# The gate's sums over partitions moved from TensorE to VectorE and a row in DRAM, and casts of late weights put behind the copies of ended banks

## The chip, the core and the metric

The kernel runs on one core of one Trainium2 chip. The metric is device time in microseconds (us) for one execution of the whole kernel. The time before is 908.64 us, the median of 3 runs (908.38 to 908.87).

## The reference

One layer of a decoder trunk is computed in float32 for a sequence of 256 tokens, 2048 model channels and a branch of 4096 channels. Written out for this case (a batch of one, one layer):

```python
h = rmsnorm(x, norm_g)                                # x: 256 x 2048
shift, scale, gate = split(silu(c) @ ada_w + ada_b, 3)  # c: 2048; ada_w: 2048 x 6144
h = h * (1 + scale) + shift
b, cg, v, g = split(h @ sc_w_in, 4)                   # sc_w_in: 2048 x 16384
u = causal_depthwise_conv(cg * v, sc_conv_w)          # three taps
y = (b * u * silu(g)) @ sc_w_out                      # sc_w_out: 4096 x 2048
out = rmsnorm(x + gate * y, final_g)
```

The vector `gate` (2048 numbers) is needed only at the end, where the output product is scaled by it. `shift` and `scale` are needed at the start, channel by channel.

## The kernel before

**Products.** Each float32 matrix is split into a high part in TensorE's reduced float32 type and the low rest, and each product is three matmuls: high by high, high by low, low by high. ScalarE makes the high part of a piece of weights (a cast, L616 in the first half of the kernel, L357 in `split` later), VectorE subtracts it from the raw piece and so makes the low part (L625, later L358). A piece is 128 x 2048 elements, 1 MB. Its raw, high and low tiles have three buffers each, so a cast waits until TensorE is through with the piece three before it.

**First half (channels 0 to 2047 of the branch, tiles `mm_s`).** `silu(c) @ ada_w` comes in pieces too, and the 16 blocks of 128 channels of `h` become ready two by two. The function `plan` (L77) writes out by hand which chunk (`ch`, 0 to 3) and which quarter (`q`, 0 to 3) of the projection is multiplied by which channels. A pass over two chunks fills two banks of PSUM, and there are three bank tiles in turn, so TensorE can begin a bank only when the bank three before it has been copied out. `keep` (L547) empties a bank: by a copy on ScalarE (L551) where it is the first part of the sum, else by an addition on VectorE (L553). The tile `acc03` holds chunk 0 and quarter 3. A loop over the pieces with a model of each engine's clock writes the program; until all of `h` is ready each engine's instructions stand in the order in which this loop issues them. For piece `b` it calls `close_bank` for the last bank that has ended and `high(b + 2)` (the cast two pieces ahead). `early` (L758) sets which of the two comes first. `low(b + 2)` (L770 or L802) follows, then the matmuls of the piece, and between a pass's two banks `close_bank` for the first (L795).

**Sums over partitions.** VectorE multiplies rows of `ada_w` by `silu(c)` and adds them up (`gv`, L484 and L486); what is left is a sum over the 128 partitions. Groups that begin at channel block 2 and 4 are turned by TensorE (`ada_turn`, L493) and summed on VectorE. Groups from 6 on are turned in 32 x 32 blocks by VectorE, summed, brought side by side and summed again (L503 to L509).

**Second half (channels 2048 to 4095, tiles `mm_b`).** Here the gate is computed beside the products, for its four parts of 512 columns one after the other (`dc`, 0 to 3). Every second piece of weights is followed by a load of a piece of `ada_w` (`gate_piece`, L834), and `gate_summed` (L855) multiplies and adds it into `gacc` on VectorE. After a part's last piece the sum over partitions is a matmul with a matrix of ones (`ones_e`), which leaves every partition with the whole sum: ScalarE takes the high part (L868), VectorE the low part (L869), TensorE runs two matmuls of 512 columns (L871), and VectorE adds the result to the bias in `gate` (L872). These instructions are traced with a later priority, and those on VectorE stand behind the low part of the next piece.

**Output stage (tiles `mm_o`).** The product with `sc_w_out` runs over four parts of 512 columns; the first three are scaled by `gate` after the product (L994), and for the fourth the weights are scaled before (L978).

Of the kernel before, what the change touches and what calls it, by code (L numbers as in the profile page):

```python
# [13 lines left out]
P = 128  # L14
# [51 lines left out]
TURN_US = 0.5  # L66
PE_TURNS = 6
TOTAL_US = 2.95
# [8 lines left out]
def plan():  # L77
# [36 lines left out]
    while new or any(k < KT for k in done.values()):  # L114
        before = []
        hi = sum(r <= pe for r in ready)
        if new:
            p = new.pop(0)
            k0 = done[p] = 0
            if p not in order:  # L120
                del done[p]
                done[order[0]] = hi
        else:
            old = [p for p in order if done[p] < KT]
            p = old[0] if hi == KT else min(old, key=lambda p: done[p])
# [30 lines left out]
def short_conv_layer(ctx: ExitStack, tc: tile.TileContext, x, c, norm_g, ada_w, ada_b, w_in, conv_w, w_out, final_g, out):  # L156
# [317 lines left out]
    def ada_sums(k0, nk, piece, at4):  # L474
# [5 lines left out]
        for i in range(kk):  # L480
# [4 lines left out]
            else:  # L485
                nc.vector.scalar_tensor_tensor(out=gv, in0=at4[:, i], scalar=c_k, in1=gv, op0=ALU.mult, op1=ALU.add)  # L486

    def ada_turn(k0, nk):

# [6 lines left out]
    def ada_total(k0, nk, tp):  # L496

        if tp is not None:
            gs = const.tile([P, 2, nk], F32, tag="gs", name="gs", bufs=2)
            nc.vector.reduce_sum(gs.rearrange("p s k -> p (s k)"), tp, axis=mybir.AxisListType.X)  # L500
            return gs[:, 0], gs[:, 1]
        tp = psum.tile([P, 512], F32, tag="sm", name="tp_g", bufs=2)
        nc.vector.transpose(tp, sums[k0].rearrange("p s f -> p (s f)"))  # L503
        nc.vector.reduce_sum(by_block, tp.rearrange("p (b j) -> p b j", j=32), axis=mybir.AxisListType.X)
        for g in range(4):
            nc.vector.tensor_copy(out=side[:, g, :], in_=by_block[32 * g : 32 * g + 32, :])
        gs = const.tile([P, 2, nk], F32, tag="gs", name="gs", bufs=2)
# [136 lines left out]
    def turn_sums(by):  # L644

        while turning and turning[0][0] < PE_TURNS and turning[0][2] <= by:
            k0, nk, _ = turning.pop(0)
            totals.append((k0, nk, ada_turn(k0, nk), clock["pe"]))

    def total_sums():  # L650

        while totals:
# [4 lines left out]
            spend("dve", FOLD_US, at)  # L657
        while turning and turning[0][0] >= PE_TURNS:
            k0, nk, _ = turning.pop(0)
# [92 lines left out]
    for b, (n, chs, q, k0, k1, seeds, w, s0, sk, _) in enumerate(flat):  # L752
# [6 lines left out]
        for closing in (early, not early):  # L759
# [4 lines left out]
            else:  # L764
                nxt = b + 2 < N and high(b + 2)
        get_ready(s0 + sk)
        if nxt:
            sum_some(nxt[2] + STALL_US, HI_US)
            if not turning or turning[0][0] >= PE_TURNS:
                low(b + 2, *nxt)  # L770
                nxt = None
# [9 lines left out]
        for j in range(len(chs)):  # L781
# [9 lines left out]
            if j == 0:  # L791
# [38 lines left out]
    gate_todo = [(dc, j) for dc in range(4) for j in range(0, KT, 2)]  # L830
    gate_held = []
    gacc = [None]
# [10 lines left out]

    def gate_sums():
        if not gate_held:
            return
        traced = nc.cur_bb.bb.instructions
        n = len(traced)
        with later(GIVE):
            gate_summed(*gate_held.pop(0))  # L850
        for ins in list(traced[n:]):
# [3 lines left out]
    def gate_summed(dc, j, at3):  # L855
# [9 lines left out]
        if j + 2 == KT:  # L865
            ps = psum.tile([P, 512], F32, tag="sm", name="ps_gate", bufs=2)
            parts = adap.tile([P, 2, 512], F32R, tag="at", name="gate_s", bufs=4)
            nc.scalar.copy(parts[:, 0], ga)  # L868
            nc.vector.tensor_tensor(out=parts[:, 1], in0=ga, in1=parts[:, 0].bitcast(F32), op=ALU.subtract)  # L869
            for i in range(2):  # L870
                nc.tensor.matmul(ps, ones_e, parts[:, i], start=i == 0, stop=i == 1)  # L871
            nc.vector.tensor_tensor(out=gate(dc), in0=ps, in1=gate(dc), op=ALU.add)  # L872

    KP = 8
    n_piece = 0
    for ct in range(NS, NCT, 2):
        for q in QUARTERS:
            bank = psum.tile([P, CT, T], F32, tag=in_turn(), bufs=1, name="mm_b")[:, 0:2]
            col = q * E + ct * P
            for kp in range(0, KT, KP):  # L880
# [12 lines left out]
                n_piece += 1  # L893
                if n_piece % 2:
                    gate_piece()
                else:
# [59 lines left out]
    for dc in range(4):  # L956
# [10 lines left out]
        for ep in range(n_ep):  # L967
# [7 lines left out]
            if dc == 3:  # L975
# [4 lines left out]
                )  # L980
            hi, lo = split(raw, SLOT, "raw")
            out_mm(po[0], 0, ep, hi, lo)
            if dc == 3 and ep >= n_ep - LATE:
# [53 lines left out]
```

## Time and profile before

| what | number |
|---|---|
| median of 3 runs | 908.64 us |
| time of the profiled execution | 908.68 us |
| span of it, first to last instruction | 906.9 us |
| TensorE busy | 893.4 us, 99% |
| VectorE busy | 643.5 us, 71% |
| ScalarE busy | 448.3 us, 49% |
| GpSimd busy | 1.8 us |
| bytes read from HBM | 224.48 MB |
| mean granted TensorE clock | 0.999 |

PE is TensorE's matmuls, PEld its weight loads, DVE is VectorE, ACT ScalarE, POOL GpSimd and SP SyncE, which issues nearly all loads. The time of a run is somewhat longer than the span, here by 1.78 us. A matmul's row gives the time from its start to its modelled end, and matmuls overlap; what one costs TensorE is read from the distance to the next start. "Idle before" with an arrow tells how long the engine had nothing to do and what ended that.

### The profile page before, as it was taken

What the parts mean: (1) busy time and instruction counts of PE and PEld (TensorE: products, weight loads), DVE (VectorE), ACT (ScalarE), POOL (GpSimd) and SP (SyncE); (2) the same over time, 40 slices, a digit from 0 to 9 for tenths busy, and PEclk for the clock granted to TensorE, in tenths of its full rate; (3) what the DMA queues carried; (4) which work ended last, traced back from release to release, by engine and by line L of the source; (5) the groups of instructions that cost most, each with busy time, mean ns of one, the idle gap of its engine ahead of it and who ended that gap; (6) DMA issues with size and microseconds to landing.
All of it is one profiled execution on the core that took longest, in us unless ns stands there. A gap on an engine that the chain in (4) does not pass through costs nothing.

```text
span 906.9 us, 16139 instructions
## 1 busy us (share of the span) xinstructions
PE 893.4 (99%) x7025; PEld 856.7 (94%) x7025; DVE 643.5 (71%) x653; ACT 448.3 (49%) x381; POOL 1.8 (0%) x8
## 2 busy tenths in 40 slices
PE   7999999999999999999999999999999999999996
PEld 4999999999999999999999999999999988888885
DVE  5788989989966868776666665657666644555882
ACT  6688755655446745544443343444333443443333
POOL 0000000000000000000000000000000000000000
PEclk9999999999999999999999999999999999999999
DMA  9999999898955566787787778777877496555542
GB/s 308 387 379 331 327 322 360 288 323 320 325 190 185 188 222 197 246 285 240 221 269 242 242 223 263 235 242 236 258 234 234 144 364 205 202 200 186 186 139 93
DMA packets 146855, 227.62 MB, mean 251 GB/s; under 512 B 5457, under 2 KB 103905, under 8 KB 146401
## 3 DMA queue, kind: packets, MB, share of 16 engines
q1 hardware_dynamic: 146688, 226.56, 74.6%
q8 instruction: 55, 0.90, 0.4%
q14 instruction: 16, 0.12, 0.0%
q0 software_dynamic: 64, 0.02, 0.0%
q10 hardware_dynamic: 32, 0.01, 0.0%
HBM read 224.48 MB, written 2.10 MB: 250 GB/s over the span
## 4 chain that ended last, share of the span: by engine, by line
PE 94%; DMA 4%; ACT 1%; SPq 0%; ACTq 0%; issue 0%; DVE 0%
PE mm_b L519 38%; PE mm_s L519 36%; PE mm_o L934 6%; PE mm_o L933 6%; PE mm_o L935 6%; DMA at<-in_ada_w_dram 3%; DMA raw_s<-in_sc_w_in_dram 1%; DMA x<-in_x_dram 1%; ACT hi L616 0%; PE ps_gate L871 0%; ACT acc L551 0%; PE tp_g L493 0%; SPq L591 0%; ACT big L947 0%; ACT big L944 0%; ACTq L1033 0%
## 5 line engine op out<-in xcount | busy, mean ns | idle before, releaser
L519 PE MATMUL mm_b<-hT,hi 128*128 128x256 f32 x2048 | 348.4, 276 | 0.0
L519 PE MATMUL mm_s<-hT,hi 128*128 128x256 f32 x2048 | 346.0, 277 | 0.6 <-ACT acc L551 0.6
L519 PEld LDWEIGHTS mm_b<-hT,hi 128*128 128x128 f32 x2048 | 308.5, 188 | 0.1
L519 PEld LDWEIGHTS mm_s<-hT,hi 128*128 128x128 f32 x2048 | 306.0, 188 | 1.0 <-ACT acc L551 0.8
L519 PE MATMUL mm_b<-hT,lo 128*128 128x256 f32 x1024 | 282.6, 276 | 0.0
L519 PE MATMUL mm_s<-hT,lo 128*128 128x256 f32 x1024 | 277.3, 276 | 0.0
L358 DVE TENSOR_TENSOR lo<-raw,hi 128x2048 fp32r<-128x2048 f32 x64 | 146.7, 2292 | 114.8 <-ACT hi L357 114.8
L357 ACT CAST hi<-raw 128x2048 fp32r<-128x2048 f32 x64 | 122.4, 1913 | 197.7 <-PE mm_b L519 145.6
L519 PEld LDWEIGHTS mm_b<-hT,lo 128*128 128x128 f32 x1024 | 192.2, 188 | 0.0
L519 PEld LDWEIGHTS mm_s<-hT,lo 128*128 128x128 f32 x1024 | 189.8, 188 | 0.0
L625 DVE TENSOR_TENSOR lo<-raw_s,hi 128x2048 fp32r<-128x2048 f32 (+1 forms) x65 | 145.3, 2239 | 38.1 <-ACT hi L616 38.0
L616 ACT CAST hi<-raw_s 128x2048 fp32r<-128x2048 f32 (+1 forms) x65 | 121.5, 1873 | 90.7 <-PE mm_s L519 70.2
L358 DVE TENSOR_TENSOR lo<-raw_o,hi 128x2048 fp32r<-128x2048 f32 x32 | 73.3, 2291 | 62.7 <-ACT hi L357 62.6
L357 ACT CAST hi<-raw_o 128x2048 fp32r<-128x2048 f32 x32 | 61.0, 1907 | 106.4 <-PE mm_o L935 84.5
L934 PE MATMUL mm_o<-lo,y 128*128 128x512 f32 x256 | 99.3, 389 | 0.0
L935 PE MATMUL mm_o<-hi,y 128*128 128x512 f32 x256 | 99.3, 389 | 0.0
L933 PE MATMUL mm_o<-hi,y 128*128 128x512 f32 x256 | 99.3, 389 | 0.0
L486 DVE SCALAR_TENSOR_TENSOR gv<-at,silu_c,gv 128x512 f32<-128x512 f32 x105 | 78.8, 750 | 3.0 <-DMA at<-in_ada_w_dram 0.3
L935 PEld LDWEIGHTS mm_o<-hi,y 128*128 128x128 f32 x256 | 48.0, 188 | 10.1
L933 PEld LDWEIGHTS mm_o<-hi,y 128*128 128x128 f32 x256 | 48.0, 188 | 10.0
L934 PEld LDWEIGHTS mm_o<-lo,y 128*128 128x128 f32 x256 | 48.0, 188 | 9.8
L551 ACT COPY acc<-mm_s 128x1024 f32<-128x1024 f32 x46 | 46.3, 1016 | 7.9 <-PE mm_s L519 7.8
(109 smaller groups left out, 373.8 us busy)
## 6 DMA issues: line engine op xcount, KB each, us to landing
raw<-in_sc_w_in_dram SPq DMA_DIRECT2D x64, 1024.0 KB, 6.4
raw_s<-in_sc_w_in_dram SPq DMA_DIRECT2D x63, 1024.0 KB, 7.1
raw_o<-in_sc_w_out_dram SPq DMA_DIRECT2D x32, 1024.0 KB, 5.1
at<-in_ada_w_dram SPq DMA_DIRECT2D x126, 256.0 KB, 7.4
at_g<-in_ada_w_dram SPq DMA_DIRECT2D x32, 512.0 KB, 7.5
x<-in_x_dram SPq DMA_DIRECT2D x4, 512.0 KB, 6.6
big<-in_x_dram SPq DMA_DIRECT2D x2, 1024.0 KB, 7.8
out_dram<-big SPq DMA_DIRECT2D x4, 512.0 KB, 2.9
```

The lines of the kernel that those rows point to most:

```text
L357: nc.scalar.copy(hi[:, :n], raw[:, :n])
L358: last_low[0] = nc.vector.tensor_tensor(out=lo[:, :n], in0=raw[:, :n], in1=hi[:, :n].bitcast(F32), op=ALU.subtract)
L486: nc.vector.scalar_tensor_tensor(out=gv, in0=at4[:, i], scalar=c_k, in1=gv, op0=ALU.mult, op1=ALU.add)
L519: mm = last_mm[0] = nc.tensor.matmul(dst, w, h[:, k], start=begins and left, stop=ends, skip_group_check=True)
L551: nc.scalar.copy(acc[ch, q], bank)
L616: nc.scalar.copy(hi[:, h], raws[b][:, h])
L625: nc.vector.tensor_tensor(out=lo[:, h], in0=raw[:, h], in1=hi[:, h].bitcast(F32), op=ALU.subtract)
L933: nc.tensor.matmul(po, yh, hi[:, o], start=opens, stop=False, skip_group_check=True)
L934: nc.tensor.matmul(po, yh, lo[:, o], start=False, stop=False, skip_group_check=True)
L935: nc.tensor.matmul(po, yl, hi[:, o], start=False, stop=ct == NCT - 1, skip_group_check=True)
```

## The change

Three things are changed.

The gate's sum over partitions no longer goes through TensorE. `block_sums`, the code that stood in `ada_total` for groups from 6 on, now also takes `gacc`: VectorE turns it in 32 x 32 blocks, sums each row of a block, and puts the four groups of partitions side by side. One more reduction (32 x 16) and one more transpose (32 x 32) leave the 512 sums as 16 rows of 32. GpSimd's queue writes these to a row in DRAM (`row`) and reads the row back into all 128 partitions (`gate_w`). The addition to `gate` is a separate step, `gate_add`, issued three pieces of weights later at the earliest (for the last part, in the output stage).

In the loop of the first half, a piece whose load is expected (by the loop's own clock) only after the first bank of the present pass has ended is marked `far`. Its cast and its low part are then issued behind the copy of that ended bank, not ahead of it.

`PE_TURNS` becomes the list (2, 4), and the plan's rule uses the number 8 where it had `PE_TURNS + 2`.

```diff
-PE_TURNS = 6
+PE_TURNS = (2, 4)
...
-            seed = k0 > 0 and (act < dve or pieces and hi > PE_TURNS + 2)
+            seed = k0 > 0 and (act < dve or pieces and hi > 8)
...
+    drams = ctx.enter_context(tc.tile_pool(name="drams", bufs=2, space=bass.MemoryType.DRAM))
...
+    total = rows1[0:32, 16:48]
+    total_t = rows1[0:32, 80:112]
...
+    def block_sums(gv):
+
+        tp = psum.tile([P, 512], F32, tag="sm", name="tp_g", bufs=2)
+        nc.vector.transpose(tp, gv)
+        nc.vector.reduce_sum(by_block, tp.rearrange("p (b j) -> p b j", j=32), axis=mybir.AxisListType.X)
+        for g in range(4):
+            nc.vector.tensor_copy(out=side[:, g, :], in_=by_block[32 * g : 32 * g + 32, :])
...
-                nxt = b + 2 < N and high(b + 2)
+                far = b + 2 < N and raws.get((b + 2, "at"), begin) > begin + us / len(chs)
+                nxt = b + 2 < N and not far and high(b + 2)
...
+                if far:
+                    nxt = high(b + 2)
+                    sum_some(nxt[2] + STALL_US, HI_US)
                 if nxt:
                     low(b + 2, *nxt)
...
-            ps = psum.tile([P, 512], F32, tag="sm", name="ps_gate", bufs=2)
-            parts = adap.tile([P, 2, 512], F32R, tag="at", name="gate_s", bufs=4)
-            nc.scalar.copy(parts[:, 0], ga)
-            nc.vector.tensor_tensor(out=parts[:, 1], in0=ga, in1=parts[:, 0].bitcast(F32), op=ALU.subtract)
-            for i in range(2):
-                nc.tensor.matmul(ps, ones_e, parts[:, i], start=i == 0, stop=i == 1)
-            nc.vector.tensor_tensor(out=gate(dc), in0=ps, in1=gate(dc), op=ALU.add)
+            block_sums(ga)
+            nc.vector.reduce_sum(total_t[:, 0:16], side.rearrange("p g b -> p b g"), axis=mybir.AxisListType.X)
+            nc.vector.transpose(total, total_t)
+            row = drams.tile([512], F32, tag="row", name="row")
+            nc.gpsimd.dma_start(row.rearrange("(b i) -> b i", b=16), total[0:16, :])
+            whole = adap.tile([P, 512], F32, tag="gv", name="gate_w")
+            nc.gpsimd.dma_start(whole, row.partition_broadcast(P))
+            gate_whole.append((dc, whole, n_piece))
+
+    def gate_add():
+
+        dc, whole, _ = gate_whole.pop(0)
+        nc.vector.tensor_tensor(out=gate(dc), in0=whole, in1=gate(dc), op=ALU.add)
```

Where this moves instructions is shown in three places.

ScalarE, near the start, before: CAST rows make the high part of a piece of weights, COPY rows empty a bank into `acc` (the two digits are chunk and quarter). `raw_s_308` is the raw tile of piece 5, `raw_s_341` that of piece 6.

```order
L551 COPY acc02_408<-mm_s_343 128x1024
L551 COPY acc12_435<-mm_s_344 128x1024
L616 CAST hi_437<-raw_s_308 128x2048
L551 COPY acc03_483<-mm_s_383 128x1024
L551 COPY acc13_510<-mm_s_410 128x1024
L616 CAST hi_512<-raw_s_341 128x2048
L551 COPY acc00_548<-mm_s_458 128x1024
L551 COPY acc10_575<-mm_s_485 128x1024
```

The same place after; piece 5 is now `raw_s_335` and piece 6 `raw_s_369`.

```order
L558 COPY acc02_398<-mm_s_339 128x1024
L623 CAST hi_401<-raw_s_292 128x2048
L558 COPY acc12_437<-mm_s_340 128x1024
L558 COPY acc03_464<-mm_s_373 128x1024
L623 CAST hi_467<-raw_s_335 128x2048
L558 COPY acc13_512<-mm_s_400 128x1024
L558 COPY acc00_539<-mm_s_439 128x1024
L623 CAST hi_542<-raw_s_369 128x2048
L558 COPY acc10_577<-mm_s_466 128x1024
```

One copy has moved ahead of each of these casts: `acc03` ahead of the cast of piece 5, `acc00` ahead of that of piece 6 (and, likewise, `acc02` ahead of piece 4 and `acc22` ahead of piece 8). Behind piece 9 the order of ScalarE's early part is as before.

TensorE, before, at the sum of the gate's first part: two matmuls of 512 columns stand among those of the second half.

```order
L519 MATMUL mm_b<-hT,lo 128x256
L519 MATMUL mm_b<-hT,hi 128x256 x2
L871 MATMUL ps_gate<-gate_s,ones 128x512
L519 MATMUL mm_b<-hT,lo 128x256
L871 MATMUL ps_gate<-gate_s,ones 128x512
L519 MATMUL mm_b<-hT,hi 128x256 x2
```

The same place after.

```order
L526 MATMUL mm_b<-hT,lo 128x256
L526 MATMUL mm_b<-hT,hi 128x256 x2
L526 MATMUL mm_b<-hT,lo 128x256
L526 MATMUL mm_b<-hT,hi 128x256 x2
L526 MATMUL mm_b<-hT,lo 128x256
```

The two `ps_gate` rows are gone, here and for the other three parts; nothing else on TensorE has moved.

VectorE, before, at the end of the gate's first part: `gate_s` is the low part for the matmul with ones; the addition (L872) stands 17 rows further down.

```order
L864 SCALAR_TENSOR_TENSOR gacc<-at_g,silu_c,gacc 128x512 x2
L358 TENSOR_TENSOR lo<-raw,hi 128x2048
L909 TENSOR_TENSOR z_4440<-z_4440 128x512
L869 TENSOR_TENSOR gate_s<-gacc,gate_s 128x512
L358 TENSOR_TENSOR lo<-raw,hi 128x2048
L862 TENSOR_SCALAR gacc<-at_g,silu_c 128x512
L864 SCALAR_TENSOR_TENSOR gacc<-at_g,silu_c,gacc 128x512
L911 TENSOR_TENSOR z_4440<-mm_b,z_4440 128x512
L358 TENSOR_TENSOR lo<-raw,hi 128x2048
L457 TENSOR_TENSOR y_4430<-z_4440,y_4430 128x2x256
```

The same place after. The block transpose of `gacc` (L494) stands right ahead of the first row; the sums go out to DRAM behind L882, and L892 is the addition of what came back.

```order
L495 TENSOR_REDUCE rows_84<-tp_g 128x16
L361 TENSOR_TENSOR lo<-raw,hi 128x2048
L497 COPY rows_84<-rows_84 32x16 x4
L931 TENSOR_TENSOR z_4442<-z_4442 128x512
L881 TENSOR_REDUCE rows_84<-rows_84 32x16
L882 STREAM_TRANSPOSE rows_84<-rows_84 32x32
L361 TENSOR_TENSOR lo<-raw,hi 128x2048
L876 TENSOR_SCALAR gacc<-at_g,silu_c 128x512
L878 SCALAR_TENSOR_TENSOR gacc<-at_g,silu_c,gacc 128x512
L933 TENSOR_TENSOR z_4442<-mm_b,z_4442 128x512
L361 TENSOR_TENSOR lo<-raw,hi 128x2048
L892 TENSOR_TENSOR gate_4439<-gate_w,gate_4439 128x512
```

Each part of the gate now has eight more small instructions on VectorE and one fewer of 128 x 512, and its addition stands two low parts behind the transpose that feeds the DRAM row.

More of the change, by code (lines that the diff above doesn't have):

```diff
@@ L501, in ada_total @@
             return gs[:, 0], gs[:, 1]
[L502 to L506, printed above, removed]
+        block_sums(sums[k0].rearrange("p s f -> p (s f)"))
         gs = const.tile([P, 2, nk], F32, tag="gs", name="gs", bufs=2)
@@ L644, in turn_sums @@
     def turn_sums(by):
-        while turning and turning[0][0] < PE_TURNS and turning[0][2] <= by:
+        while turning and turning[0][0] in PE_TURNS and turning[0][2] <= by:
             k0, nk, _ = turning.pop(0)
@@ L657, in total_sums @@
             spend("dve", FOLD_US, at)
-        while turning and turning[0][0] >= PE_TURNS:
+        while turning and turning[0][0] not in PE_TURNS:
             k0, nk, _ = turning.pop(0)
@@ L768, in short_conv_layer @@
             sum_some(nxt[2] + STALL_US, HI_US)
-            if not turning or turning[0][0] >= PE_TURNS:
+            if not turning or turning[0][0] not in PE_TURNS:
                 low(b + 2, *nxt)
@@ L830, in short_conv_layer @@
     gate_todo = [(dc, j) for dc in range(4) for j in range(0, KT, 2)]
-    gate_held = []
+    gate_held, gate_whole = [], []
     gacc = [None]
@@ L842, in gate_piece, with gate_sums @@
         gate_held.append((dc, j, at3))
-    def gate_sums():
-        if not gate_held:
+    def gate_sums(add=False):
+        if not (gate_whole if add else gate_held):
             return
@@ L849, in gate_sums @@
         with later(GIVE):
-            gate_summed(*gate_held.pop(0))
+            if add:
+                gate_add()
+            else:
+                gate_summed(*gate_held.pop(0))
         for ins in list(traced[n:]):
@@ L894, in short_conv_layer @@
                 if n_piece % 2:
+                    if gate_whole and n_piece >= gate_whole[0][2] + 3:
+                        gate_sums(add=True)
                     gate_piece()
@@ L981, in short_conv_layer @@
             hi, lo = split(raw, SLOT, "raw")
+            if dc == 0 and ep == 1:
+                gate_sums(add=True)
             out_mm(po[0], 0, ep, hi, lo)
```

## The prediction

> **What bounds the kernel now.** I read the page first: its span, and the engines' shares in the chain that ended last.
>
> ```profile
> span 906.9 us, 16139 instructions
> PE 94%; DMA 4%; ACT 1%; SPq 0%; ACTq 0%; issue 0%; DVE 0%
> ```
>
> The chain is TensorE. The table by stage (us busy of TensorE, its weight loads, VectorE, ScalarE and GpSimd, then the granted clock, the share of the DMA engines and GB/s) says how full it is, and TensorE's list of waits what is left.
>
> ```profile
> 45.00:272.00 227.00, 226.92 (x2001) 226.93 (x2002) 201.94 (x252) 142.23 (x115) 0.00 (x0) 1.00 0.90 317
> sum 855.00, PE 854.71 PEld 824.02 DVE 612.41 ACT 415.87 POOL 0.00; mean PE 213.68 PEld 206.01 DVE 153.10 ACT 103.97 POOL 0.00
> ...
> PE tp_v L275 <- DMA rows<-in_c_dram: 4.0, 1, 4.0
> PE tp_x L342 <- ACT x L336: 1.7, 2, 1.4
> PE mm_s L519 <- ACT acc L551: 0.6, 1, 0.6
> ```
>
> Over the 855 us from 45 to 900 TensorE is busy 854.71 us. Outside the start-up it waits once, for a copy of a bank. So time is won by matmuls taken away, by that one wait, or not at all; other engines count only where they make TensorE wait. The one wait, in TensorE's timeline:
>
> ```profile
> 43.85 0.28 PE L519 MATMUL mm_s<-hT,lo 128*128 128x256 f32 x1
> ...
> 44.19 0.28 PE L519 MATMUL mm_s<-hT,lo 128*128 128x256 f32 x1
> 45.08 0.51 PE L519 MATMUL mm_s<-hT,hi 128*128 128x256 f32 x2 [0.61 <-ACT acc L551]
> 45.42 0.28 PE L519 MATMUL mm_s<-hT,lo 128*128 128x256 f32 x1
> ```
>
> A group of three matmuls takes 44.19 - 43.85 = 0.34 us; this one took 45.42 - 44.19 = 1.23. The wait costs 0.89 us, more than the 0.61 of its row, since matmul ends are modelled. ScalarE's timeline shows why:
>
> ```profile
> 37.02 1.93 ACT L551 COPY acc<-mm_s 128x1024 f32<-128x1024 f32 x2
> 42.20 1.91 ACT L616 CAST hi<-raw_s 128x2048 fp32r<-128x2048 f32 x1 [3.25 <-DMA raw_s<-in_sc_w_in_dram]
> 44.02 1.93 ACT L551 COPY acc<-mm_s 128x1024 f32<-128x1024 f32 x2
> 45.83 1.93 ACT L616 CAST hi<-raw_s 128x2048 fp32r<-128x2048 f32 x1
> ```
>
> ScalarE stood 3.25 us before the cast of piece 5, whose load had not landed, while a bank that had ended waited behind it for its copy (44.02, `acc03`).
>
> **The change part by part.** *The eight matmuls.* The chain at the first part of the gate, and at the fourth:
>
> ```profile
> 489.96 3.52 PE mm_b L519 x31
> 493.48 0.23 PE ps_gate L871
> 493.71 0.12 PE mm_b L519
> 493.83 0.23 PE ps_gate L871
> 494.06 6.01 PE mm_b L519 x53
> ...
> 747.19 0.47 PE ps_gate L871 x2
> ```
>
> From 493.48 to 494.06 are 0.58 us; without the product between them (6.01 / 53 = 0.113) a pair costs 0.467 us. The fourth pair has 0.47. TensorE does not wait around them, so all of it is on the path: 4 x 0.467 = 1.87 us. Their weight loads are within these distances.
>
> *The early copies.* A bank of a full piece is 24 matmuls, 24 x 0.113 = 2.72 us. TensorE stopped at 44.31 (44.19 and one step), between the two banks of a pass, so the bank of `acc03`, three back, had ended two banks earlier, at 38.9. In the new order its copy stands ahead of the cast of piece 5 and runs at about 38.9 to 39.9, in the time in which ScalarE waited. TensorE goes on at 44.31 and 0.89 us are won. What is late next is the second cast. Behind the cast of piece 5 (done at 44.02, as before, for its load is the same) now come `acc13` and `acc00` (0.96 each, half of 1.93), so piece 6's cast starts at 45.9 against 45.83. The low part of piece 5 is nearest:
>
> ```profile
> 44.15 2.29 DVE L625 TENSOR_TENSOR lo<-raw_s,hi 128x2048 fp32r<-128x2048 f32 x1
> ...
> 48.14 0.28 PE L519 MATMUL mm_s<-hT,lo 128*128 128x256 f32 x1
> ```
>
> It ends at 46.44 and TensorE first takes it at 48.14; with 0.89 gone that is 47.25, still 0.81 later. The wait's 0.89 could also be lost at the next place where TensorE and VectorE meet, the turn of the group from channel block 4 (its reduction follows at once):
>
> ```profile
> 95.29 0.69 DVE L500 TENSOR_REDUCE gs<-tp_g 128x4 f32<-128x512 f32 x1 [0.92 <-PE tp_g L493]
> ```
>
> VectorE was idle 0.92 us before it, just enough if VectorE itself were to gain nothing. The bounds of this term are 0 and 0.89 us. Below 0 the room of 0.81 just shown speaks against it. I take 0.89, since each cover is there in a row.
>
> *What moves with it.* On SyncE's queue the load of piece 10 now stands ahead of one piece of `ada_w`, which may come one load of 1 MB later, at the 317 GB/s of the first stage's row 3.3 us. Such pieces are not what VectorE waits for:
>
> ```profile
> DVE gv L486 <- DMA at<-in_ada_w_dram: 0.3, 1, 0.3
> ```
>
> Cost 0; without that cover it is 3.3 us once, at the turn of a group. `PE_TURNS` takes the same groups (2 and 4) by another spelling, and 8 is 6 + 2: nothing.
>
> *VectorE's new work.* The nearest rows, by line:
>
> ```profile
> L503 DVE STREAM_TRANSPOSE tp_g<-gv 128x512 f32<-128x512 f32 x5 | 3.6, 720 | 0.0
> L504 DVE TENSOR_REDUCE rows<-tp_g 128x16 f32<-128x512 f32 x5 | 3.4, 689 | 0.1
> L509 DVE TENSOR_REDUCE gs<-rows 32x4 f32<-32x16 f32 x20 | 3.4, 171 | 0.4
> L506 DVE COPY rows<-rows 32x16 f32<-32x16 f32 x20 | 3.3, 163 | 0.3
> L869 DVE TENSOR_TENSOR gate_s<-gacc,gate_s 128x512 fp32r<-128x512 f32 x4 | 2.7, 686 | 0.0
> ```
>
> Per part 0.72 + 0.69 + 4 x 0.163 = 2.06 us, and two instructions which the trace does not show: the 32 x 16 reduction lies between 0.171 and 0.689 (16 times the elements of the one, a quarter of the other's per partition in 64 against 512), the 32 x 32 transpose between 0.163 and 0.72. I take 0.25 and 0.2, near the small rows. Less the 0.69 of `gate_s` that is 1.8 us more per part, at most 2.8. The addition costs the same as before and only moves. The cover, in VectorE's and ScalarE's timelines at the first part:
>
> ```profile
> 453.68 2.29 DVE L358 TENSOR_TENSOR lo<-raw,hi 128x2048 fp32r<-128x2048 f32 x1 [1.70 <-ACT hi L357]
> 455.89 0.69 DVE L909 TENSOR_TENSOR z<-z 128x512 f32<-128x512 f32 x1
> ...
> 464.56 2.29 DVE L358 TENSOR_TENSOR lo<-raw,hi 128x2048 fp32r<-128x2048 f32 x1 [1.19 <-ACT hi L357]
> 466.77 0.69 DVE L457 TENSOR_TENSOR y<-z,y 128x512 fp32r<-128x512 f32 x1
> 470.00 2.29 DVE L358 TENSOR_TENSOR lo<-raw,hi 128x2048 fp32r<-128x2048 f32 x1 [2.54 <-ACT hi L357]
> ```
> ```profile
> 468.06 1.91 ACT L357 CAST hi<-raw 128x2048 fp32r<-128x2048 f32 x1 [3.01 <-issue]
> 473.50 1.91 ACT L357 CAST hi<-raw 128x2048 fp32r<-128x2048 f32 x1 [3.53 <-PE mm_b L519]
> ```
>
> The casts come one per piece (5.44 us = 48 x 0.113), each when TensorE has left the piece three before (three buffers), so TensorE reaches the piece cast at 468.06 two pieces on, at 478.9. Its low part ended at 472.3: 6.6 us to spare. The transpose and first reduction (1.41) fit into the 1.70 us idle ahead of 453.68; the rest delays the next low part by a fraction of 6.6. Cost 0.
>
> *The way through DRAM.* This is the wait that is added: the addition (L892) waits for the second of two DMAs, and behind it on VectorE stand the low part of `y` and that of the next piece (470.00), for which TensorE waits. GpSimd's own DMAs at the start, issue to landing, and the loads beside which the new ones run:
>
> ```profile
> DMA to landing us min/median/max: 5.7/5.7/5.7
> ...
> DMA to landing us min/median/max: 6.6/6.6/6.6
> ...
> at_g<-in_ada_w_dram SPq DMA_DIRECT2D x32, 512.0 KB, 7.5
> ```
>
> The sums are ready behind 453.68: low part, copies, product, reduction and transpose end at about 457.7. Two DMAs at 5.7 to 7.5 us take 11.4 to 15; I take 13, between them. The row is back at 470.7, the addition would have been reached at 466.8, so VectorE stands about 4 us. Then 0.69 + 0.69 + 2.29 for addition, `y` and low part: 474.4, against 478.9. The point from which TensorE waits is 478.9 - 3.7 - 457.7 = 17.5 us for both DMAs. Cost 0, at both ends of the range. GpSimd's queue holds nothing else then (POOL 0.00 in the sum row).
>
> [...]
>
> **The sum.** Against the profiled execution: 908.68 - 1.87 - 0.89 = 905.92 us, of which the span is 904.1 and 1.78 lie around it. The median of the runs, 908.64, is 0.04 below that execution, so 905.9 stands for a median as well.
>
> **The rivals.**
>
> *The early gain is given back* (13%). The 0.89 us is lost again at 47 or 95 us. For it: room of only 0.81 and 0.92. Against it: both are at least near 0.89, and VectorE's low parts follow casts that TensorE releases, so it gains too. Time: 908.68 - 1.87 = 906.8.
>
> *The row comes back late* (5%), the case on the other side. If each of the two DMAs takes 7.5 us, as the loads do, and is begun only when VectorE has ended the low part in hand (2.29), the two take 19.6 us, 2.1 beyond the point of 17.5, and TensorE waits in each of four parts: 905.9 + 8.4 = 914.3. It is slower than before from 17.5 + 2.76 / 4 = 18.2 us on. [...] Against: it takes 9 us for each DMA, above all three rows. [...]
>
> *The change doesn't do what it says* (2%): the gate's matmuls turn out to have filled gaps, and their time stays. Against it: 854.71 of 855. Time: 908.68 - 0.89 = 907.8.
>
> **How the numbers follow.** The forecast, both gains with the path kept clear, has 80%. The measurement can tell 0.2% of 908.64, or 1.82 us, from no change, so "faster" ends at 906.82. The forecast is beyond that; the first rival lies right on it and is halved, and the third is no change that shows. Faster 0.86, same 0.09, slower 0.05. The range goes from 905.3 (0.6 of unforeseen easing, as large as the listed wait) to 907.1 (the second case and 0.3 for the spread of the runs and small stands).
>
> **What would show it.** In the new profile TensorE should have eight matmuls fewer and no wait on `acc` near 44; the second half should be shorter by three pairs (1.40) and the output stage by one (0.47). The addition L892 should wait a few us for `gate_w`, with no wait of TensorE behind it. Wrong would be: a TensorE wait for `lo` near 47 or 95 us; one for `hi` or `lo` some 20 us behind each DRAM row; DMAs of GpSimd beyond 8 us each.

## The result and the profile after

The changed kernel takes 905.42 us (median of 6 runs, 905.19 to 905.85) against 908.79 for the kernel before beside it (908.38 to 909.68): 3.37 us less, ratio 0.9963 with the interval 0.995 to 0.9975. It is faster, as forecast; the 905.9 of the forecast is 0.5 too high. The profiled execution took 905.36 us, 3.32 below the 908.68 of before. The ranges below leave out one execution of the kernel before that fell in a slower state (1000.61 us, at a granted clock of 0.851).

The page's head of the changed kernel, the engines' shares in its chain, and the queue of GpSimd's DMAs:

```profile
span 903.6 us, 16165 instructions
PE 890.8 (99%) x7017; PEld 854.8 (95%) x7017; DVE 650.7 (72%) x681; ACT 446.3 (49%) x377; POOL 6.1 (1%) x16
...
q0 software_dynamic: 512, 1.08, 0.4%
...
PE 98%; DMA 1%; ACT 1%; DVE 0%; SPq 0%; ACTq 0%; issue 0%; DVEq 0%
```

TensorE has 8 matmuls fewer (7017 against 7025) and is 98% of the chain, where it was 94%. The starts of its matmuls in the two profiles say where the time went: the second half begins at 374.10 us where it was 375.45 (1.35 less), lasts 348.16 us where it was 349.58 (1.42 less; 1.40 was forecast for three pairs of matmuls), and the output stage is 0.51 us shorter (0.47 was forecast for one pair). VectorE works 7.2 us more (643.5 before), which is 1.8 per part of the gate, and none of it is in the chain.

The first stage in the table by stage (columns as before), and TensorE's whole list of waits:

```profile
45.00:272.00 227.00, 227.00 (x2005) 227.00 (x2004) 203.09 (x254) 142.57 (x115) 0.00 (x0) 1.00 0.91 318
```
```profile
PE tp_v L276 <- DMA rows<-in_c_dram: 4.1, 1, 4.1
PE tp_x L345 <- ACT x L339: 1.4, 2, 1.2
```

Both waits are of the start-up. The one for `acc` is gone and none has come in its place. ScalarE's timeline at that place:

```profile
38.61 1.02 ACT L558 COPY acc<-mm_s 128x1024 f32<-128x1024 f32 x1 [0.63 <-PE mm_s L526]
42.26 1.92 ACT L623 CAST hi<-raw_s 128x2048 fp32r<-128x2048 f32 x1 [2.64 <-DMA raw_s<-in_sc_w_in_dram]
44.08 1.93 ACT L558 COPY acc<-mm_s 128x1024 f32<-128x1024 f32 x2
45.88 1.93 ACT L623 CAST hi<-raw_s 128x2048 fp32r<-128x2048 f32 x1
```

The copy of `acc03` (38.61) now runs in the time in which ScalarE stood before the cast of piece 5. The load is as late as before, the cast starts at 42.26 against 42.20, and piece 6's cast at 45.88 against 45.83.

VectorE's timeline, first the turn of the group from channel block 4, then the first part of the gate, and the addition of the fourth:

```profile
93.94 0.69 DVE L511 TENSOR_REDUCE gs<-tp_g 128x4 f32<-128x512 f32 x1 [0.92 <-PE tp_g L504]
...
455.88 0.25 DVE L881 TENSOR_REDUCE rows<-rows 32x16 f32<-32x64 f32 x1
456.16 0.20 DVE L882 STREAM_TRANSPOSE rows<-rows 32x32 f32<-32x32 f32 x1
457.73 2.29 DVE L361 TENSOR_TENSOR lo<-raw,hi 128x2048 fp32r<-128x2048 f32 x1 [1.37 <-ACT hi L360]
...
463.17 2.29 DVE L361 TENSOR_TENSOR lo<-raw,hi 128x2048 fp32r<-128x2048 f32 x1 [1.14 <-ACT hi L360]
468.17 0.69 DVE L892 TENSOR_TENSOR gate<-gate_w,gate 128x512 f32<-128x512 f32 x1 [2.71 <-DMA gate_w<-row]
468.78 0.68 DVE L460 TENSOR_TENSOR y<-z,y 128x512 fp32r<-128x512 f32 x1
469.39 2.29 DVE L361 TENSOR_TENSOR lo<-raw,hi 128x2048 fp32r<-128x2048 f32 x1
...
730.88 0.69 DVE L892 TENSOR_TENSOR gate<-gate_w,gate 128x512 f32<-128x512 f32 x1 [3.71 <-DMA gate_w<-row]
```

The turn comes at 93.94, 1.35 us earlier than the 95.29 of before, and VectorE still stands 0.92 ahead of it: it has gained as much as TensorE. At the gate's part VectorE stands 2.71 us for the row (3.71 at the fourth). The low part behind it ends at 471.7.

GpSimd's timeline, first and last part, shows the way through DRAM:

```profile
456.65 0.49 POOL L884 DMA_DIRECT2D row<-rows  x1 [454.08 <-DVE rows L882]
462.06 0.57 POOL L886 DMA_DIRECT2D gate_w<-row  x1 [4.92 <-DMA row<-rows]
...
717.76 0.50 POOL L884 DMA_DIRECT2D row<-rows  x1 [80.86 <-DVE rows L882]
722.66 0.56 POOL L886 DMA_DIRECT2D gate_w<-row  x1 [4.40 <-DMA row<-rows]
```

From the first issue to the addition's start are 11.5 us (456.65 to 468.17) and 13.1 us (717.76 to 730.88); the two parts between have 11.4 and 12.0.

### The profile page after: what moved, and what is told of

It is laid out like the page before. It is cut to its first block, busy times and chain, and to the rows that moved or that the text cites. A ratio compares the mean times of both kernels' runs of the same rounds, so it can differ in the third digit from the quotient of the medians.

```text
span 903.6 us, 16165 instructions
## 1 busy us (share of the span) xinstructions
PE 890.8 (99%) x7017; PEld 854.8 (95%) x7017; DVE 650.7 (72%) x681; ACT 446.3 (49%) x377; POOL 6.1 (1%) x16
## 4 chain that ended last, share of the span: by engine, by line
PE 98%; DMA 1%; ACT 1%; DVE 0%; SPq 0%; ACTq 0%; issue 0%; DVEq 0%
PE mm_s L526 39%; PE mm_b L526 39%; PE mm_o L955 6%; PE mm_o L957 6%; PE mm_o L956 6%; DMA x<-in_x_dram 1%; PE sum L376 1%; PE tp_x L345 0%; ACT x L339 0%; DVE junk L320 0%; SPq L239 0%; PE tp_idle L290 0%; PE tp_x L290 0%; PE tp_g L504 0%; ACT big L969 0%; ACT big L966 0%
```

## The experiments

Each ran beside the kernel before on the same chip. Where a kernel changes the program of before it is called so; the others change the changed kernel. None leaves out part of the computation; the added matmuls write a tile that nothing reads.

| run | median us | lowest to highest | ratio to before, interval |
|---|---|---|---|
| gate_only | 906.69 | 906.12 to 906.91 | 0.9977, 0.9968 to 0.9986 |
| far_only | 907.19 | 906.94 to 907.84 | 0.9985, 0.9976 to 0.9994 |
| before_again | 908.63 | 907.83 to 909.04 | 0.9998, 0.9989 to 1.0008 |
| idle_before | 908.59 | 908.24 to 908.95 | 0.9999, 0.999 to 1.0007 |
| idle_after | 905.5 | 905.42 to 905.56 | 0.9964, 0.9951 to 0.9978 |
| pad_before | 908.62 | 908.31 to 909.17 | 0.9997, 0.9987 to 1.0007 |
| pad_after | 906.29 | 905.97 to 906.63 | 0.9975, 0.9965 to 0.9984 |
| hops1 | 913.49 | 912.91 to 914.08 | 1.0052, 1.0038 to 1.0066 |
| hops2 | 921.1 | 919.38 to 923.98 | 1.0139, 1.012 to 1.0158 |
| hops1_late | 906.0 | 905.31 to 906.32 | 0.9972, 0.996 to 0.9983 |
| turn4 | 917.61 | 916.91 to 918.25 | 1.01, 1.0086 to 1.0113 |
| turn4_in_place | 906.3 | 905.83 to 906.62 | 0.997, 0.996 to 0.998 |

**Which part brings what.** The theory: matmuls 1.87 us and early copies 0.89, which add. The measured 3.37 is 0.61 more than that sum, so one term is larger. The gate's part alone, in the changed kernel:

```diff
-                far = b + 2 < N and raws.get((b + 2, "at"), begin) > begin + us / len(chs)
+                far = False
```

> The change without its second part: no piece is ever marked far, so ScalarE's, VectorE's and SyncE's early orders are those of before, and only the gate's sums are new. My theory (the parts add): TensorE's eight matmuls are gone (4 x 0.467 = 1.87 us) and the wait near 44 us with its 0.89 us is there again, so 1.9 us under the kernel before: 906.8, ratio 0.9979. The rival (the way through DRAM costs TensorE something that the early part pays for): less than 1.5 us under the kernel before. Of the 0.5 us that the changed kernel gained beyond the sum, the profiles show a slower pace of TensorE from 27 to 39 us in before only (0.1178 us a matmul against 0.1133): if it belongs to the early order of before, this run's profile shows 0.1178 there; if it belongs to the one execution, it shows either.

The early order alone, put into the kernel before (`high` makes the cast, `low` the low part, `sum_some` gives VectorE some of its sums in between):

```diff
-                nxt = b + 2 < N and high(b + 2)
+                far = b + 2 < N and raws.get((b + 2, "at"), begin) > begin + us / len(chs)
+                nxt = b + 2 < N and not far and high(b + 2)
...
+                if far:
+                    nxt = high(b + 2)
+                    sum_some(nxt[2] + STALL_US, HI_US)
```

> The kernel before with the second part alone: late casts behind the ended banks' copies, the gate's sums as before. My theory: the wait near 44 us is gone and nothing takes its place, 0.89 us under the kernel before: 907.8, ratio 0.9990. The rival (the wait moves to the low part near 47 us or to the turn at 95 us): no gain, ratio 1.000. If the slower pace of TensorE from 27 to 39 us belongs to the early order of before, it is gone here as well and the gain is 1.36 us: 907.4, ratio 0.9985.

And the kernel before once more, with no edit, for a second profile of it:

> The kernel before, unchanged, profiled once more and timed against itself: ratio 1.000, and the width of its interval is what these rounds can tell. If the slower pace of TensorE from 27 to 39 us belongs to that kernel, this profile shows 0.1178 us a matmul there again and the wait of 0.89 near 44; if it belongs to one execution, it shows 0.1133 there and a span shorter by up to 0.5 us.

Against the 908.63 of before in these runs, gate_only takes 1.94 us less and far_only 1.44 less. Together 3.38, the 3.37 measured: the parts add. The matmuls are as forecast (1.87); the early order is worth more than 0.89, though the interval of far_only alone (0.5 to 2.2 us) would still allow that, and the profiles of the two kernels have 1.35. TensorE's timeline in before_again, at the wait:

```profile
43.36 0.28 PE L519 MATMUL mm_s<-hT,lo 128*128 128x256 f32 x1
45.08 0.50 PE L519 MATMUL mm_s<-hT,hi 128*128 128x256 f32 x2 [1.44 <-ACT acc L551]
45.41 0.28 PE L519 MATMUL mm_s<-hT,lo 128*128 128x256 f32 x1
```

By the prediction's reckoning (45.41 - 43.36 - 0.34) the same program waits 1.71 us here, where its first profile had 0.89. TensorE comes back at 45.08 in both; it *arrived* 0.83 earlier (last matmul at 43.36, not at 44.19). The span is 906.9 us as in the first profile, and not shorter by up to 0.5 as the expectation had it: what the faster pace won went into the wait. In gate_only:

```profile
43.96 0.28 PE L526 MATMUL mm_s<-hT,lo 128*128 128x256 f32 x1
45.21 0.50 PE L526 MATMUL mm_s<-hT,hi 128*128 128x256 f32 x2 [0.97 <-ACT acc L558]
45.55 0.28 PE L526 MATMUL mm_s<-hT,lo 128*128 128x256 f32 x1
```

That is 1.25, ended at 45.21. The end of the wait stays, its start moves from execution to execution. In the changed kernel TensorE starts the matmul that stood behind the wait (the 169th into `mm_s`) at 43.85:

```profile
43.85 0.39 PE L526 MATMUL mm_s<-hT,hi 128*128 128x256 f32 x2
```

The prediction had 44.31 for it, read from the one profile of before. In the seven profiles with the new order and no added matmul (the changed kernel, far_only, and hops1, hops1_late, hops2, turn4 and turn4_in_place below) it lies between 43.45 and 44.11, so that one profile showed an arrival later than all of these, and a shorter wait. A part of why, in the table by stretches of TensorE alone (busy and count, granted clock, DMA), 28 to 38 us, of the kernel before:

```profile
28.00:38.00 10.00, 10.00 (x87) 1.00 1.06 372
```

of far_only:

```profile
28.00:38.00 10.00, 10.00 (x88) 1.00 1.07 374
```

of before_again:

```profile
28.00:38.00 10.00, 10.00 (x90) 1.00 1.05 369
```

and of the changed kernel:

```profile
28.00:38.00 10.00, 10.00 (x91) 1.00 1.06 376
```

TensorE is busy all the time at the same recorded clock, but 87 matmuls fall into this stretch in one execution and 90 in the other of the same program; by the distances of their starts, 0.118 us each against 0.113. The order of the copies doesn't set this pace: far_only has the new order and 88, before_again the old one and 90.

**Is the wait's end tied to the load?** The chain of before says so up to this point, for it holds nothing of TensorE between 22.5 and 45.08:

```profile
32.55 9.58 DMA raw_s<-in_sc_w_in_dram
...
42.20 1.91 ACT hi L616
44.12 0.92 ACT acc L551
...
45.08 16.60 PE mm_s L519 x144
```

If piece 5's load, its cast and the copy behind it end the wait whenever TensorE arrives, then a later arrival costs the kernel before nothing and the changed kernel all of it. First, three idle matmuls more (of 512 columns) ahead of the first product, in each kernel:

```diff
-    IDLE = (2, 2, 3, 2, 2, 2, 1, 1)
+    IDLE = (2, 2, 3, 2, 2, 2, 1, 4)
```

> The kernel before with three more idle matmuls of 512 columns right ahead of TensorE's first product (IDLE's last number 4 for 1), about 0.7 us (3 x 0.23) more work on TensorE at 24 us, before the wait near 44. My theory now: that wait ends when piece 5's load has landed and been cast (TensorE goes on near 45.1 in each of before's three profiles with that order), however early TensorE comes there, so TensorE comes 0.7 us later, waits 0.7 us less, and the time stays: 908.6, ratio 1.000. The rival (the wait is a fixed price of 0.9 us): 0.7 us slower, 909.3, ratio 1.0008.

> The changed kernel with the same three idle matmuls. My theory: nothing behind them waits on TensorE's path any more, so all of it shows: 905.4 + 0.7 = 906.1, 0.7 us less gain over the kernel before than the changed kernel has. The rival (something else pinned to a load holds the first half of the changed kernel too): less than 0.3 us shows.

The kernel before stays at 908.59. The changed kernel went to 905.5, only 0.1 up: my expectation was wrong. Its first product starts 0.40 later (24.84 against 24.44), but three stops of about 0.1 us between 24.4 and 27.2 us are gone. Two of them ended just when VectorE had made a low part of `hT` (25.43 and 26.88), so the first pass is held by VectorE as well. So the pair of medians decides nothing, and the delay has to be put further on. But the profile of idle_before has something to say: its load landed earlier, the cast began at 41.81 (42.20 in before), and the wait ended at 44.68.

```profile
44.68 0.51 PE L519 MATMUL mm_s<-hT,hi 128*128 128x256 f32 x2 [0.68 <-ACT acc L551]
```

That is 0.40 earlier than in before, though TensorE's first product came 0.35 later, and this execution took 908.26 us, 0.42 less than the profiled one of before. For the test, four matmuls of 512 columns (0.91 us, at the step of 0.227 that such matmuls have in the output stage) are put at piece 3, about 36 us:

```diff
+        if b == 3:
+            pad = psum.tile([P, 512], F32, tag="sm", name="pad", bufs=2)
+            for _ in range(4):
+                nc.tensor.matmul(pad, ones_r[:, 0:P], ones_r, start=True, stop=True, skip_group_check=True)
```

> The kernel before with four matmuls of 512 columns more (into a tile that nobody reads) ahead of TensorE's fourth pass, near 36 us: 0.91 us (4 x 0.227) more work, between the start and the wait near 44. My theory: TensorE goes on when piece 5's load has landed and been cast, near 45.1, so the work goes into the wait: of 0.9 to 1.6 us (three profiles with that order) 0.9 are filled, and the time stays within 0.2 us of before, 908.6, ratio 1.000. The rival (the wait has a fixed price): 0.9 us slower, 909.5, ratio 1.0010.

> The changed kernel with the same four matmuls at the same place. My theory: nothing behind them is pinned to a load, so all 0.91 us show: 906.3. With the run above, the early part's gain is then what TensorE can do ahead of the load, and not a fixed number. The rival (the changed kernel too is held by a load or by VectorE in the first half): under 0.4 us shows.

The kernel before with the pad takes 908.62, as without; the changed kernel 906.29, 0.87 more; the slowest run of the changed kernel (905.85) is faster than the fastest with the pad (905.97). A fixed price would have been 909.5 for the kernel before, above its slowest run with the pad (909.17). The wait of pad_before, in TensorE's timeline:

```profile
44.83 0.28 PE L519 MATMUL mm_s<-hT,lo 128*128 128x256 f32 x1
45.14 0.51 PE L519 MATMUL mm_s<-hT,hi 128*128 128x256 f32 x2
45.48 0.28 PE L519 MATMUL mm_s<-hT,lo 128*128 128x256 f32 x1
```

It has shrunk to 0.31 us (45.48 - 44.83 - 0.34) and ends at 45.14. So the wait's end is tied to the load, and the wait hides what delays TensorE ahead of it, up to its own length: 0.9 us of extra matmuls here, a slower pace there. (The waits of 0.9 to 1.6 in the expectation are 0.89 to 1.71 by the reckoning used here.)

**When does the row come back too late?** The forecast had 17.5 us for the way through DRAM as the point from which TensorE waits; 11.4 to 13.1 were measured, so the point was not reached. One and two copies of the row within DRAM make the way longer:

```diff
+HOPS = 1
...
+            for _ in range(HOPS):
+                copy = drams.tile([512], F32, tag="row", name="row")
+                nc.gpsimd.dma_start(copy.rearrange("(b i) -> b i", b=16), row.rearrange("(b i) -> b i", b=16))
+                row = copy
...
-        nc.vector.tensor_tensor(out=gate(dc), in0=whole, in1=gate(dc), op=ALU.add)
+        last_add.append(nc.vector.tensor_tensor(out=gate(dc), in0=whole, in1=gate(dc), op=ALU.add))
```

The last line and one in `split` (not shown) hold the addition ahead of the next low part that is traced behind it, so that the compiler's scheduler doesn't move it. hops2 has `HOPS = 2`.

> The changed kernel with one more copy of the row from DRAM to DRAM between the write and the read back, and the addition held ahead of the same low part as in the changed kernel: three DMAs on the way, some 5.4 + 5 + 6.2 = 16.6 us where two took 11.5. My theory: the addition then waits some 7 us on VectorE, which is still inside the 17 to 18 us that the low part behind it has, so the time is that of the changed kernel, 905.4, and TensorE has no wait. The rival (the way through DRAM already costs TensorE something): slower than the changed kernel by a part of 4 x 5 us.

> The same with two more copies: four DMAs, some 21.8 us. My theory: the low part behind the addition is now late, by 21.8 - 18 = some 4 us in each of four parts, and TensorE waits for it: 905.4 + 15 = 920 (913 to 927), and the profile shows four waits of TensorE for a low part. The rival (VectorE's three buffers of low parts cover any such wait): 905.4.

hops1 took 913.49, where 905.4 was expected. In its first three parts the way took 16.1, 15.9 and 17.0 us, and TensorE did not wait: the low part behind the addition ended 2.09, 2.26 and 1.10 us before it was taken. VectorE's timeline at the first part:

```profile
465.15 0.68 DVE L463 TENSOR_TENSOR y<-z,y 128x512 fp32r<-128x512 f32 x1
472.48 0.69 DVE L899 TENSOR_TENSOR gate<-gate_w,gate 128x512 f32<-128x512 f32 x1 [6.64 <-DMA gate_w<-row]
473.08 2.29 DVE L362 TENSOR_TENSOR lo<-raw,hi 128x2048 fp32r<-128x2048 f32 x1
```

So the point lies near 18.1 us with this order (16.1 + 2.09, 15.9 + 2.26, 17.0 + 1.10). But here the low part of `y` (465.15) stands ahead of the addition, where the changed kernel has it behind (468.78), and it takes 0.6. In the changed kernel the low part ends at 471.68 and is taken at 477.68: its point is the way of 11.5 and these 6.0, 17.5, as forecast. The time of hops1 went at the fourth part, where my edit held the addition one piece earlier than the changed kernel does. TensorE's wait, and the table by stretches there (columns as before):

```profile
PE mm_o L963 <- DVE lo L362: 4.8, 1, 4.8
```
```profile
726.00:732.00 6.00, 6.00 (x28) 4.97 (x27) 0.00 (x0) 1.90 (x1) 0.56 (x1) 1.00 0.98 396
732.00:738.00 6.00, 1.31 (x6) 0.75 (x4) 2.82 (x3) 0.00 (x0) 0.00 (x0) 0.88 0.87 315
738.00:744.00 6.00, 5.87 (x15) 4.63 (x16) 4.54 (x3) 1.90 (x1) 0.00 (x0) 0.55 0.76 261
744.00:750.00 6.00, 6.00 (x29) 4.94 (x28) 1.91 (x1) 1.90 (x1) 0.00 (x0) 1.00 0.74 266
```

Behind the wait the granted clock is 0.55 in a stretch of 6 us and only 15 matmuls fall into it where 28 did: in the records it is 0.5 from 736.5 to 743.4. TensorE starts no matmul from 732.93 to 738.14, 5.0 us more than its usual step of 0.23, so 5.2 of the 6.8 us at half the clock fall on work and cost half of that (the starts at 738.72, 739.15 and 739.58 are 0.43 apart). The sum, 5.0 + 2.6 = 7.6, is what the two profiled executions differ by (912.91 and 905.36); the medians differ by 8.1. Half the clock also followed shorter waits: in hops2 one of 1.89 us by its row (2.06 by the matmuls' starts), and in turn4 one of 2.7 (2.9).

hops2 took 921.1, with waits in all four parts:

```profile
PE mm_o L963 <- DVE lo L362: 7.6, 1, 7.6
PE mm_b L529 <- DVE lo L362: 5.0, 3, 1.9
```

The first three parts have ways of 20.1, 19.5 and 20.1 us; beyond a point of 18.1 that is 2.0, 1.4 and 2.0, 5.4 in all. They waited 5.0 by their rows, 5.5 by the matmuls' starts. The total is near the 920 expected, but partly by luck: some 4 us were expected in each part, and the first three had less and the fourth more, with half the clock behind it. With the addition of the fourth part held where the changed kernel has it:

```diff
-            if dc == 0 and ep == 1:
+            if dc == 0 and ep == 2:
```

> Three DMAs on the way again, with the fourth part's addition held ahead of the low part of the output stage's piece 3, where the changed kernel has it, and not of piece 2 as in the run before. My theory: the 4.8 us wait of that run came from this place alone, and with one piece (5.4 us) more room all four parts have the 17 us that they need: 905.4 to 905.8, TensorE's only wait at most 0.3 us, and no dip of the granted clock. The rival (three DMAs are too slow for the output stage in any place): 908 or more.

hops1_late takes 906.0, 7.5 less than hops1, by one place in VectorE's order. TensorE's list of waits has the start-up alone, and VectorE's timeline shows that the fourth row came as late as in hops1 (addition at 735.18 there):

```profile
PE tp_v L277 <- DMA rows<-in_c_dram: 4.5, 1, 4.5
```
```profile
735.17 0.69 DVE L899 TENSOR_TENSOR gate<-gate_w,gate 128x512 f32<-128x512 f32 x1 [8.26 <-DMA gate_w<-row]
```

It is on the edge: the low part behind the addition ends at 738.06, and TensorE takes it at 738.42. The median is 0.6 above the changed kernel's, and where that goes isn't settled: the profiled execution, 905.31, was the fastest of its runs and doesn't show it.

**Can one more turn leave TensorE?** The same block transposes could take channel block 2's group off TensorE (0.5 us of transposes):

```diff
-PE_TURNS = (2, 4)
+PE_TURNS = (4,)
```

> The changed kernel with the list of groups that TensorE turns cut to (4,), so that the four transposes of the group from channel block 2 go to VectorE as well (seven small instructions more there near 62 us, 2.7 us). If what TensorE does is paid in full and what VectorE does is free, the time falls by what these transposes cost in the profile (3.08 + 2.86 us for two banks with the turn in them, 5.44 without: 0.5 us) to 904.9. The rival (near 62 us VectorE is the narrow place, and the channel blocks 2 and 3 or the low part near 68 us come late): 905.4 or more, with a wait of TensorE near 68 us.

It took 917.61, 12.2 more than the changed kernel. TensorE's wait, and one stretch behind it:

```profile
PE mm_s L526 <- ACT hT L352: 6.7, 2, 4.0
```
```profile
100.00:106.00 6.00, 5.51 (x24) 5.34 (x25) 3.63 (x5) 1.83 (x3) 0.00 (x0) 0.50 0.97 335
```

The loop charges this turn 2.95 us, and its reckoning then puts later groups in another order: TensorE stands twice (4.73 and 2.99 us by its matmuls' starts). Half the clock follows for 6.8 us, 5.6 of them after TensorE is back at work, and for 3.4 us. The sum, 4.73 + 2.99 + (5.6 + 3.4) / 2 = 12.2, less 0.5, is 11.7, near the 11.9 by which the profiled executions differ. So the run prices the reordering, not the turn. If VectorE's clock in the loop is charged for this turn as for one on TensorE, the later order stays: TensorE's four transposes go, ten small instructions of VectorE come for one, and one low part now stands ahead of the turn instead of behind it:

```diff
-            spend("dve", TOTAL_US)
+            spend("dve", FOLD_US if k0 == 2 else TOTAL_US)
```

> The changed kernel with the four transposes of the group from channel block 2 moved from TensorE to VectorE, as in the run before, but with VectorE's clock in the loop charged for them as for the old way (0.75 and not 2.95 us), so that all later instructions stand where the changed kernel has them. In the run before TensorE had no wait near 68 us; its 4.7 us at 95.8 and 3.0 us at 228 came, by my theory, from the order that the longer charge made of the later groups. Then both waits are gone and the four transposes' 0.5 us are won: 904.9, and VectorE's 2 us more near 65 us lie in its idle time up to 95 us. The rival (VectorE has no 2 us to give before the turn at 93 us): a wait of TensorE there, and 906 or more.

It took 906.3, 0.9 more than the changed kernel; the rival of that expectation came true. TensorE's one new wait, and what it waits for on ScalarE:

```profile
PE mm_s L526 <- ACT mm_s L709: 0.5, 1, 0.5
```
```profile
90.33 1.02 ACT L709 COPY mm_s<-acc 128x1024 f32<-128x1024 f32 x1 [2.10 <-DVE acc L560]
```

VectorE's longer turn makes its addition to `acc` late (89.08 to 90.30), ScalarE's copy of that into a bank stands 2.10 us for it, and TensorE behind it. By the starts of the matmuls, compared one by one with the changed kernel's, 0.5 is saved at the turn, 0.4 is lost again in steps of about 0.1 between 68 and 82 us (their cause is open), and 0.8 at the wait; the rest of the difference lies ahead of the turn. The changed kernel is the fastest version tried.

## Why the prediction held, and the term that was mis-sized

- *What bounds the kernel.* Right: time came only from matmuls removed and from the one wait. 7.2 us more on VectorE cost nothing. But "The chain is TensorE" passed over the 4% of DMA in it, which is the chain's way to 45.08 and says that the one wait is pinned to a load.
- *The eight matmuls.* 1.87 forecast, 1.94 in gate_only, and 1.93 between the profiles of the two kernels (1.42 + 0.51).
- *The early copies.* The mechanism was right (cast of piece 6 at 45.9 forecast, 45.88 found; the copy at 38.9, found at 38.61), the size was not. The term that was mis-sized is "TensorE goes on at 44.31 and 0.89 us are won", with 0.89 as the upper bound. The wait's end is fixed by a load; its start by all that TensorE did from the first product on, which differs between executions of one program (0.89 and 1.71 us in two profiles of the kernel before). The term measured 1.44 in far_only, by difference 3.37 - 1.94 = 1.43, and 1.35 between the profiles of the two kernels, all above that bound. The miss of the gain, 3.37 against 2.76, is 0.55 from this term and 0.07 from the matmuls. That the result still lies in the range, 0.1 from its lower end, is partly luck: the 0.6 us below the sum were set aside for unforeseen easing, and the reason given for their size was only the wait row's 0.6. That the wait absorbs such differences is shown by the pads: 0.0 before, 0.87 after.
- *The early gain given back (13%).* It wasn't. The turn came 1.35 earlier with VectorE still idle 0.92 before it. The reason given, that VectorE's work is released by TensorE and gains with it, fits that row.
- *VectorE's new work.* The two durations taken between bounds (0.25 and 0.2) were measured at 0.25 and 0.20; 1.8 us per part, as summed. The comparison in brackets is off (an input of 32 x 64 is four times one of 32 x 16, and 64 elements per partition are an eighth of 512), but nothing hangs on it.
- *The way through DRAM.* 13 us taken from 11.4 to 15; measured 11.4 to 13.1. VectorE stood 2.6 to 3.7 us, about 4 forecast. TensorE's point was put at 17.5, and it lies there in the changed kernel's order (18.1 in that of hops1). The rival's condition, more than 9 us for each DMA, did not arise: the longest took 8.2 from issue to landing.
- *The rival's price* was too low: 2.1 us per part, taken as the wait alone. In hops2's first three parts, waits of 5.5 us in all (by the matmuls' starts) made the second half 7.6 us longer than in the changed kernel, since half the clock followed one of them; the 5.0 of hops1 cost 7.6.
- *GpSimd's issues beside VectorE.* The rival had each DMA begun only when VectorE has ended the low part in hand. No run here shows such a delay. In the changed kernel GpSimd's issues took 0.49 to 0.57 us, but most of them fell into pauses of VectorE (456.65 lies between the transpose's end at 456.36 and the low part at 457.73). Two in other runs lie wholly inside a low part: in gate_only (551.72, the low part from 551.70 to 553.99) the issue took 0.56 and the landing came 4.93 after its start, in hops2 (463.46, the low part from 463.43 to 465.72) 0.49 and 4.46, no more than the others.

## What to carry to other kernels

The wait that a load ended was an absorber here: four added matmuls (0.91 us) ahead of it cost nothing, and 0.87 us where it was gone. Its length in one profile said how late the engine happened to arrive, and removing it was worth the distance from the engine's own arrival to the end of the load's chain (0.89 and 1.71 us in the two profiles of the kernel before, 1.44 measured in far_only). That arrival differed by 0.8 us between two profiles of one program here, so take it from more than one and allow more than one shows. Work taken off the bounding engine was worth its full time here (1.94 us in gate_only, 1.87 reckoned), where that engine had no wait behind it, and the detour that replaces it, 11.4 to 13.1 us, was free below a point (17.5) that could be reckoned from the next consumer. A move of one row in a waiting engine's order can decide: hops1 and hops1_late differ by 7.5 us, by the place of one addition alone.

## What the runs showed of the hardware

TensorE's pace between 28 and 38 us varied by 4% between executions of one program (87 and 90 matmuls in 10 us), busy throughout, at a granted clock recorded as 1.00. It isn't the order of the copies (far_only has 88 with the new order). What sets it is open.

Behind the start-up, waits of TensorE up to 1.44 us by their rows (before_again; 1.26 in hops2) were followed by no loss of granted clock. Those of 2.7 us and more were followed by half the clock for 3.4, 6.8 or 10.2 us (turn4, hops1, hops2). Of two waits of 1.89 us in hops2, one was followed by 3.4 us of it and one by none. For the three longest waits half the clock began 3.5 to 3.6 us after TensorE's last matmul into the product had started, so while TensorE still stood (hops1: last start at 732.93, half the clock from 736.52, next start at 738.14). The part of it that fell on work was 3.4 to 5.9 us, so such a wait cost its length and 1.7 to 2.9 us more.

A copy of 2 KB within DRAM, issued by GpSimd beside the loads, took 5.0 to 5.7 us from issue to landing in hops1, nearly as much as the 4.4 to 7.2 us of the row's spread over 128 partitions behind it.
